# Queueing the first loads of the down projection in order of need, ahead of the last stores of the gate and up projections

## The chip, the cores and the metric

The kernel runs on one core of a Trainium2 chip. The metric is the device time of one execution in microseconds (us), the median of three runs. Besides it there is the profile of one execution; the times in its rows count from the start of its span.

## The reference, cut to what matters

One layer of a hybrid encoder: half a SwiGLU block, a mixing stage (attention beside a recurrent group), and half a SwiGLU block again. 1024 rows of a prompt and 64 rows of running streams go through together (1088 tokens, width 1024). What the change touches is the passage between the two halves of each SwiGLU block:

```python
def swiglu(x, w_gate, w_up, w_down):                 # 1024 -> 2816 -> 1024
    return (jax.nn.silu(x @ w_gate) * (x @ w_up)) @ w_down
x = x + 0.5 * swiglu(rms_norm(x, norm_ffn1), ffn1_gate, ffn1_up, ffn1_down)
...
x = x + 0.5 * swiglu(rms_norm(x, norm_ffn2), ffn2_gate, ffn2_up, ffn2_down)
```

## The kernel before, in words

Every product is made with operands split into a high and a low part (three passes of the matrix engine), and the two SwiGLU blocks use a seven-product scheme of the Winograd kind on 2x2 blocks, so each block of work has seven products where the plain one would have eight.

**Gate and up** (`gate_up`, lines 281 to 486). The seven combinations of the normalised input lie in SBUF as S0 to S6, each with a high and a low tile, in a pool on the right side of SBUF. 22 matrices are worked off, gate and up by turns; each takes its seven products in the order S0, S5, S4, S6, S1, S2, S3 (`UNIT`, line 225), 24 matmuls of 272 columns per product. `after` takes the results out of PSUM; after an up matrix the finished hidden pair is combined, split and stored to DRAM (`store`, to `hcd` and `hsd`). The last pair has no partner and is stored by `store_rows` (lines 436 to 450) to `hd`: for each of two halves one DMA of `hi` (line 448), one of `hs` (449) and one of `gt` (450).

**Down** (`Down`, lines 495 to 681). It runs over 5 groups of 7 blocks. A block needs one tile of hidden values `h` (1 MB, tags ha to he in rotation, `load_h`), one weight unit `wh`, made on chip by a cast (ScalarE) and a subtraction (VectorE) from a raw tile `dr` of 2 MB per group (two DMAs, `load_raw`) or from sums of its parts that GpSimd makes (lines 550 to 556), and, in blocks 0, 1, 3 and 4, the rows of the streams `hs` (0.25 MB per group, `load_hs`). A block is 24 matmuls of 512 columns, 28 with `hs`. Its results are added to the residual tiles x0 to x8 (`load_x`, 0.5 MB each, 0.25 MB for x8). The units lie in a ring of six: two in `whb` on the right, four in `whl` on the left. The weights of the last pair (`wr`, line 137) are loaded by the same `refill`.

**The turn.** In the last product of the last matrix (n = 6, S3) `run` of the matrix calls `last()`, which builds `Down`: it closes the pool of S and lays its own buffers where S was, so a load must wait for the last product that reads the S tiles beneath its buffer (a wait per tile, `reuse_waits="tile"`). Then come `after`, `store_rows`, the closing of gate_up's pools on the left, and `Down.run`, which lays further buffers where these were.

**What sets the order.** The program is written in one sequence, and a planner at build time simulates it and fixes the order on each engine: what it believes to be ready first is issued first. All loads and stores here are issued by SP, which takes them strictly in that order: an issue that waits for its data or its buffer holds back those behind it. Nothing in the kernel before ties the loads at the turn to each other or to the stores.

**Where the buffers lie.** The pools on the right grow from the high end downwards, and the first tile of a pool lies lowest. From the tile sizes (S: 8.5 KB per partition each, x: 4, dr: 16, h: 8, hs: 2):

| buffer | before: over | after: over |
|---|---|---|
| dr of group 0, dt | S5, S0 | S5, S0 |
| ha (h0) | S4, S5 | S4 |
| hb (h1) | S4 | S4, S2 |
| hc (h2) | S3, S4 | S2 |
| hs | gt and p1 (left side) | S4, S5 |
| x0, x1 | S0 | S0 |
| x8, x2 | S0 and S2, S2 | S1, S1 |
| x3 | S2 | S3, S1 |
| x4 to x7 | S2, S2 and S1, S1, S1 | S3 (x4 also S0) |
| hd, he (h3, h4) | gt, hi | hl, p1 (split weights) |
| dr of group 1 | hl, p1 | gt, p1 |
| whb | S6, S1 | S6, S1 |

The functions that the change touches, and those that call them:

Of the kernel before, what the change touches and what calls it, by code (L numbers as in the profile page):

```python
# [37 lines left out]
def rows(t):  # L38
    return 128 if t < 8 else NS


def build(tc, I, O):
# [15 lines left out]
    def left(name, bufs=1, **k):  # L58
        return Pool(name, bufs, side="left", reuse_waits="tile", **k)

    def right(name, bufs=1, **k):
        return Pool(name, bufs, side="right", reuse_waits="tile", **k)
# [30 lines left out]
    def bits(ap):  # L93
        return ap.bitcast(F32)
# [134 lines left out]

    def new_s(pool):  # L230
        made = {i: tuple(pool.tile([128, 4, 2, CW], F32R, tag=f"S{i}{b}") for b in "hl")
                for i in (3, 4, 5, 0, 2, 1, 6)}
        return [made[i] for i in range(7)]

    def build_s(p, a, b, S7, tmp, eng=None):
# [45 lines left out]
    def gate_up(tag, S7, turn, first=None, go=None):  # L281
# [62 lines left out]
        class Matrix:  # L344
# [51 lines left out]
            def run(self, ns, last=None):  # L396
                for n in ns:
                    product(*self.begin(n))
                    if n == 6 and last:
                        last()  # L400
                    self.after(n)
                if self.kind == "u":
                    (self.store if self.i < 2 * NG else self.store_rows)()

            def store(self):

# [88 lines left out]
    class Down:  # L495
        def __init__(self, tag, sP, keys, src):

            self.tag, self.src, self.w = tag, src, I["d" + tag]
            sP.close()
            open_ring(keys)  # L500
            self.xp = right("xd")
            self.right = [right(n) for n in ("dr", "dt", "dh")]
            rr, self.tp, hr = self.right
            self.raws, self.t, self.h, self.hs = {}, {}, {}, {}
            self.rawp, self.hp = {0: rr}, dict.fromkeys("abc", hr)
            ring["blocks"] = self.blocks
            order_x = (0, 1, 8, 2, 3, 4, 5, 6, 7)
            x = {t: self.xp.tile([128, D], tag=f"x{t}") for t in order_x}
            self.x = [x[t] for t in range(NT)]
            for i in (2, 1, 0):  # L510
                self.h_tile(i)
            self.load_raw(0)
            self.load_h(0)
            refill(1)
            self.load_h(1)
            refill(2)
            G.memset(self.x[8][NS:128], 0.0)
            for t in order_x[:5]:
                self.load_x(t)
            self.load_h(2)  # L520

        def load_x(self, t):
            SP.dma_start(self.x[t][:rows(t)], self.src[t * 128:t * 128 + rows(t), :])

        def load_raw(self, g):
            if g < NG:
                r = self.raws[g] = self.rawp[g % 2].tile([128, 2, 4, 512], tag="dr")
                for i in range(2):
                    SP.dma_start(r[:, i], self.w[2 * g + i])

        def h_tile(self, k):
            tag = "abcde"[k % 5]
# [2 lines left out]
        def load_h(self, k):  # L535
            if k < 7 * NG:
                if k not in self.h:
                    self.h_tile(k)
                SP.dma_start(bits(self.h[k]), hcd[k // 7, k % 7])

        def load_hs(self, g):
            if g < NG:
                h = self.hs[g] = self.hsp.tile([128, 4, 128], F32R, tag="hs", bufs=2)
                SP.dma_start(bits(h), hsd[g])

        def blocks(self, tag, g, i):
            r = self.raws[g]
# [13 lines left out]
        def run(self):  # L561
            x = self.x
            open_rest()
            self.left = [left(n) for n in ("dl", "ds", "de")]
            self.rawp[1], self.hsp, hl = self.left
            self.hp.update(dict.fromkeys("de", hl))
            vw = right("vw")
            acc = {n: [vw.tile([128, 512], tag=f"{n}{p}") for p in range(4)] for n in "vw"}
            ps = Pool("pw", 8, space=PSUM, reuse_waits="tile")
            self.load_hs(0)  # L570
            self.load_h(3)
            refill()
            self.load_h(4)
            for t in (4, 5, 6, 7):
                self.load_x(t)

            def bank():
                return ps.tile([128, 512], tag="pw")

            def add(out, p, scale, first=False):  # L580
                if first:
                    S.activation(out=out, in_=p, func=AF.Copy, scale=scale)
                else:
                    V.scalar_tensor_tensor(out=out, in0=p, scalar=scale, in1=out, op0=OP.mult, op1=OP.add)  # L584

            lo, hi = slice(0, 512), slice(512, 1024)

            def evac(g, i, p, q):
                v, w = acc["v"][p], acc["w"][p]
                if i == 0:  # L590
                    add(v, q, 0.5, g == 0)
                elif i == 1:
                    add(x[p][:, lo], q, 0.5)
                elif i == 2:
                    add(v, q, 0.5)
                elif i == 3:
                    add(w, q, 0.5, g == 0)
                elif i == 4:
                    add(x[p][:, hi], q, 0.5)
                elif i == 5:  # L600
                    add(w, q, -0.5)
                else:
                    add(x[p + 4][:, lo], q, 0.5)

            def sample(g, i, q):
                if i == 0:
                    add(x[8][:, hi], q, -0.5)
                elif i == 1:
                    add(x[8][:, lo], q, 0.5)
                elif i == 4:  # L610
                    add(x[8][:, hi], q, 0.5)

            for g in range(NG):
                self.load_hs(g + 1)
                for i in range(7):
                    h, u = self.h.pop(7 * g + i), units["s", self.tag, g, i]
                    begins = i in (0, 2, 3, 5)
                    if begins:
                        qs = {}
                    row = {0: 0, 1: 1, 3: 0, 4: 1}.get(i)  # L620
                    for p in [0, 1, 2, 3] + ([4] if row is not None else []):
                        if begins:
                            qs[p] = bank()
                        if p < 4:
                            seq = [(h[:, r, a, p * 128:p * 128 + 128], u[:, b, r * 512:r * 512 + 512])
                                   for r in range(2) for a, b in PASSES]
                        else:
                            seq = [(self.hs[g][:, 2 * r + row], u[:, b, r * 512:r * 512 + 512])
                                   for r in range(2) for b in range(2)]
                        for j, (l, m) in enumerate(seq):  # L630
                            PE.matmul(qs[p], l, m, start=begins and j == 0, stop=j == len(seq) - 1,  # L631
                                      skip_group_check=not begins)
                        if p < 4:
                            evac(g, i, p, qs[p])
                        else:
                            sample(g, i, qs[p])
                    del units["s", self.tag, g, i]
                    self.load_h(7 * g + i + 5)
                    refill()
                    if g == NG - 1 and i == 2:  # L640
                        for p in range(4):
                            G.tensor_tensor(out=x[p][:, hi], in0=x[p][:, hi], in1=acc["v"][p], op=OP.subtract)
                        for p in range(4):
                            G.tensor_tensor(out=x[p + 4][:, lo], in0=x[p + 4][:, lo], in1=acc["v"][p], op=OP.add)
                    if g == NG - 1 and i == 5:
                        for p in range(4):
                            G.tensor_tensor(out=acc["w"][p], in0=acc["w"][p], in1=acc["v"][p], op=OP.subtract)
                            G.tensor_tensor(out=x[p + 4][:, hi], in0=x[p + 4][:, hi], in1=acc["w"][p], op=OP.add)
                del self.hs[g]
            ps.close()  # L650
            for p in [vw] + self.right[::-1] + self.left[::-1]:
                p.close()
# [133 lines left out]
    def turn1():  # L786
        down[1] = Down("1", sP, down_keys("1") + [("r", j) for j in range(8)]
                       + [(p, j) for p in "kqv" for j in range(4)] + [("o", j) for j in (4, 5, 6, 7, 0, 1, 2, 3)],
                       I["x"])

    gate_up("1", S7, turn1, first1)
    d1 = down[1]
# [597 lines left out]

    def turn2():
        down[2] = Down("2", sP, down_keys("2"), xd)

    gate_up("2", S7, turn2, go=rest)
    d2 = down[2]
# [123 lines left out]
```

## Time and profile before

| | |
|---|---|
| time, median of 3 runs | 2104.07 us (2102.86 to 2110.48) |
| the profiled execution: its time | 2107.18 us |
| its span | 2105.3 us |
| TensorE busy | 1943.2 us (92%) |
| VectorE, ScalarE, GpSimd busy | 1416.7, 842.0, 756.0 us |
| mean granted TensorE clock | 0.968 of full |
| moved by DMA | 328.92 MB, mean 156 GB/s |
| the turns of the two SwiGLU blocks | about 518 us and 1823 us |

How to read the rows: PE is the matrix engine, PEld its weight loads, DVE is VectorE, ACT ScalarE, POOL GpSimd, SPq the queue of SP. A timeline row gives start, duration, engine, line, operation, output<-input and how many were merged; in square brackets the idle time of the engine before it and what ended that. [...]

### The profile page before, as it was taken

Reading aid. Unit: us, or ns where it says so; the run is one execution under the profiler, and the core shown is the slowest. Engines: PE = TensorE matmul, PEld = TensorE weight load, DVE = VectorE, ACT = ScalarE, POOL = GpSimd, SP = SyncE. Lnnn points to the kernel's source line nnn. Section 1 sums busy time; section 2 is a strip of 40 time slices with the busy share of each in tenths; the row PEclk is TensorE's granted clock in tenths of the full one; section 3 lists DMA queues with packets and bytes.
Section 4 is the critical chain, followed back from the end, with each engine's and each line's share of the span. In section 5 each row is a group of like instructions: output and inputs, shape, how many; then the busy total and the mean of one; then the engine's idle time right before and its main releaser. Section 6 shows DMA issues by size and latency. Waiting matters only on the chain.

```text
span 2105.3 us, 32015 instructions
## 1 busy us (share of the span) xinstructions
PE 1943.2 (92%) x12260; PEld 1764.9 (84%) x12260; DVE 1416.7 (67%) x2420; ACT 842.0 (40%) x1604; POOL 756.0 (36%) x561
## 2 busy tenths in 40 slices
PE   4999999998499999998998988799999999749999
PEld 3999999998388879986876866699999999738887
DVE  7777677665367767168944877866677767437774
ACT  7534344443121124356762766544344434221110
POOL 5654444442312151013121422454444444322213
PEclk9999999999699999998999999899999999979999
DMA  3243344333965552214369953333344333485652
GB/s 127 82 158 139 114 162 150 139 113 128 362 227 217 180 178 101 83 57 129 104 191 249 179 125 100 125 125 142 113 162 150 139 113 145 166 332 220 226 211 85
DMA packets 130812, 328.92 MB, mean 156 GB/s; under 512 B 19074, under 2 KB 73762, under 8 KB 112995
## 3 DMA queue, kind: packets, MB, share of 16 engines
q1 hardware_dynamic: 109922, 312.45, 42.0%
q0 software_dynamic: 20736, 14.42, 4.2%
q8 instruction: 97, 1.59, 0.3%
q14 instruction: 57, 0.46, 0.1%
HBM read 208.85 MB, written 117.98 MB: 155 GB/s over the span
## 4 chain that ended last, share of the span: by engine, by line
PE 49%; DMA 5%; DVE 5%; ACT 3%; issue 1%; SPq 0%; ACTq 0%; DVEq 0%
PE pq L331 22%; PE pw L631 10%; PE pg L219 5%; PE pg L1046 4%; PE pd L675 2%; PE T L1234 2%; PE T L1223 2%; PE S L1175 1%; DMA x<-xd 1%; DMA hs<-hsd 1%; DMA ot<-od 1%; DMA hb<-hcd 1%; PE T L1208 1%; DVE xs L197 1%; DMA hd<-gt 1%
## 5 line engine op out<-in xcount | busy, mean ns | idle before, releaser
L420 DVE TENSOR_TENSOR hi<-gt,hi 128x512 fp32r<-128x512 f32 x140 | 165.1, 1179 | 40.4 <-ACT hi L419 38.7
L98 DVE TENSOR_TENSOR hl<-t,hl 128x512 fp32r<-128x512 f32 x132 | 106.9, 810 | 125.7 <-ACT hl L97 124.6
L98 DVE TENSOR_TENSOR hl<-raw,hl 128x512 fp32r<-128x512 f32 x176 | 170.3, 969 | 9.6 <-ACT hl L97 9.5
L584 DVE SCALAR_TENSOR_TENSOR x<-pw,x 128x512 f32<-128x512 f32 x150 | 101.7, 688 | 111.2 <-PE pw L631 110.7
L97 ACT CAST hl<-raw 128x512 fp32r<-128x512 f32 x176 | 108.9, 621 | 117.9 <-PE pq L331 76.9
L419 ACT CAST hi<-gt 128x512 fp32r<-128x512 f32 x140 | 85.4, 621 | 167.5 <-DMA hcd<-hi 90.5
L331 PE MATMUL pq<-S0h,hl 128*128 128x272 f32 x704 | 143.3, 292 | 5.2 <-ACT hl L97 4.2
L331 PE MATMUL pq<-S1h,hl 128*128 128x272 f32 x704 | 140.4, 288 | 3.2 <-ACT p L463 3.2
L1046 PE MATMUL pg<-wh,xh 128*128 128x512 f32 (+1 forms) x432 | 140.3, 404 | 0.0
L331 PE MATMUL pq<-S5h,hl 128*128 128x272 f32 x704 | 139.9, 288 | 0.0
L331 PE MATMUL pq<-S4h,hl 128*128 128x272 f32 x704 | 139.5, 287 | 0.0
L331 PE MATMUL pq<-S6h,hl 128*128 128x272 f32 x704 | 139.4, 287 | 0.0
L331 PE MATMUL pq<-S2h,hl 128*128 128x272 f32 x704 | 139.4, 287 | 0.0
L331 PE MATMUL pq<-S3h,hl 128*128 128x272 f32 x704 | 139.4, 287 | 0.0
L331 PEld LDWEIGHTS pq<-S0h,hl 128*128 128x128 f32 x704 | 115.7, 192 | 5.9 <-ACT hl L97 4.6
L331 PEld LDWEIGHTS pq<-S1h,hl 128*128 128x128 f32 x704 | 113.6, 188 | 3.8 <-ACT p L463 3.8
L331 PEld LDWEIGHTS pq<-S5h,hl 128*128 128x128 f32 x704 | 113.5, 188 | 0.0
L331 PEld LDWEIGHTS pq<-S6h,hl 128*128 128x128 f32 x704 | 113.3, 188 | 0.0
L331 PEld LDWEIGHTS pq<-S4h,hl 128*128 128x128 f32 x704 | 113.3, 188 | 0.0
L331 PEld LDWEIGHTS pq<-S3h,hl 128*128 128x128 f32 x704 | 113.3, 188 | 0.0
L331 PEld LDWEIGHTS pq<-S2h,hl 128*128 128x128 f32 x704 | 113.3, 188 | 0.0
L304 POOL TENSOR_TENSOR t<-t,raw 128x512 f32<-128x512 f32 x44 | 58.8, 1336 | 133.3 <-DVE hl L98 133.3
(285 smaller groups left out, 5531.7 us busy)
## 6 DMA issues: line engine op xcount, KB each, us to landing
hcd<-hi SPq DMA_DIRECT2D x140, 512.0 KB, 2.7
raw<-in_g SPq DMA_DIRECT2D x22, 1024.0 KB, 6.1
raw<-in_u SPq DMA_DIRECT2D x22, 1024.0 KB, 5.0
dr<-in_d SPq DMA_DIRECT2D x20, 1024.0 KB, 8.3
ha<-hcd SPq DMA_DIRECT2D x14, 1024.0 KB, 4.8
hb<-hcd SPq DMA_DIRECT2D x14, 1024.0 KB, 4.8
hc<-hcd SPq DMA_DIRECT2D x14, 1024.0 KB, 4.9
hd<-hcd SPq DMA_DIRECT2D x14, 1024.0 KB, 4.8
```

Source lines behind the costliest of these rows:

```text
L97: S.copy(out=hi, in_=raw)
L98: (eng or V).tensor_tensor(out=lo, in0=raw, in1=bits(hi), op=OP.subtract)
L219: PE.matmul(p[:, :n], w[:, a, k, :], x2[b][:, k, o:o + n], start=i == 0, stop=i == 23)
L304: G.tensor_tensor(out=t2, in0=t2, in1=r[:, 2], op=OP.add)
L331: PE.matmul(q[:, c, :CW], h[:, a, k * 128:k * 128 + 128], S7[i][b][:, k, c, :], start=start and j == 0, stop=j == 11, skip_group_check=not ...
L419: S.copy(out=hi, in_=v)
L420: V.tensor_tensor(out=lo, in0=v, in1=bits(hi), op=OP.subtract)
L584: V.scalar_tensor_tensor(out=out, in0=p, scalar=scale, in1=out, op0=OP.mult, op1=OP.add)
L631: PE.matmul(qs[p], l, m, start=begins and j == 0, stop=j == len(seq) - 1, skip_group_check=not begins)
L675: PE.matmul(p, l, r, start=i == 0, stop=i == len(seq) - 1)
L1046: PE.matmul(ps[:n], x2[b][:, 2 * j + kk, ts], w[:, a, kk, :], start=half == 0 and i == 0, stop=half == 1 and i == 11)
L1223: PE.matmul(po[:n, :128], aT[:kw, i, :n], v[:kw, vi[i], :], start=i == 0, stop=i == nk - 1)
```

## The change

The loads of `Down.__init__` and the first of `Down.run` go through a new method `queue`, which ties each to the one before by `tc.issue_after`: it sets the order of issue on SP and adds no wait for the earlier transfer. The order is dr (two), h0, hs, x0, x1, h1, x8, x2, x3 in `__init__`, then h2, h3, h4, x4 to x7 in `run`. The last load of `__init__` is handed back as `gate`, and `store_rows` is traced under `issue_after(gate)`, so its six DMAs are issued behind x3's load. From then on (`ordered = False`) loads are as free as before; the first full `refill`, with the load of dr of group 1, is moved behind x4 to x7. `hs` goes to the right side, `dl` and `de` on the left change places, the order of the S tiles and of the x tiles in memory changes (table above). No instruction of arithmetic is added or taken away.

```diff
     def new_s(pool):
...
-                for i in (3, 4, 5, 0, 2, 1, 6)}
+                for i in (2, 4, 5, 0, 3, 1, 6)}
...
                     if n == 6 and last:
-                        last()
+                        gate = last()
                     self.after(n)
-                if self.kind == "u":
-                    (self.store if self.i < 2 * NG else self.store_rows)()
+                if last:
+                    with tc.issue_after(gate):
+                        self.store_rows()
+                elif self.kind == "u":
+                    self.store()
...
-            self.right = [right(n) for n in ("dr", "dt", "dh")]
-            rr, self.tp, hr = self.right
+            self.right = [right(n) for n in ("dr", "dt", "ds", "dh")]
+            rr, self.tp, self.hsp, hr = self.right
...
-            order_x = (0, 1, 8, 2, 3, 4, 5, 6, 7)
-            x = {t: self.xp.tile([128, D], tag=f"x{t}") for t in order_x}
+            x = {t: self.xp.tile([128, D], tag=f"x{t}") for t in (0, 1, 4, 5, 6, 7, 3, 8, 2)}
...
+            self.gate = None
             self.load_raw(0)
             self.load_h(0)
             refill(1)
+            G.memset(self.x[8][NS:128], 0.0)
+            self.load_hs(0)
+            for t in (0, 1):
+                self.load_x(t)
             self.load_h(1)
             refill(2)
-            G.memset(self.x[8][NS:128], 0.0)
-            for t in order_x[:5]:
+            for t in (8, 2, 3):
                 self.load_x(t)
-            self.load_h(2)
+
+        def queue(self, out, src):
+
+            if not self.ordered:
+                return SP.dma_start(out, src)
+            if self.gate is None:
+                self.gate = SP.dma_start(out, src).ins
+                return
+            with tc.issue_after(self.gate):
+                i = SP.dma_start(out, src)
+            self.gate = i.ins
...
-            self.left = [left(n) for n in ("dl", "ds", "de")]
-            self.rawp[1], self.hsp, hl = self.left
+            self.left = [left(n) for n in ("de", "dl")]
+            hl, self.rawp[1] = self.left
...
-            self.load_hs(0)
+            self.load_h(2)
             self.load_h(3)
-            refill()
             self.load_h(4)
             for t in (4, 5, 6, 7):
                 self.load_x(t)
+            self.ordered = False
+            refill()
```

In `load_x`, `load_raw`, `load_h` and `load_hs` the call `SP.dma_start` becomes `self.queue`. `turn1` and `turn2` return `down[1].gate` and `down[2].gate`.

## Rows read from the trace of the kernel before

**Rows 1.** The page, busy time of TensorE over the span, and its granted clock in 40 slices of the span, in tenths.
```profile
PE 1943.2 (92%) x12260; PEld 1764.9 (84%) x12260; DVE 1416.7 (67%) x2420; ACT 842.0 (40%) x1604; POOL 756.0 (36%) x561
...
PEclk9999999999699999998999999899999999979999
```

**Rows 2.** Busy time by windows around the first turn: from:to, length, then PE, PEld, DVE, ACT, POOL busy us with the count of instructions, granted clock, DMA share, GB/s.
```profile
500.00:550.00 50.00, 32.02 (x193) 28.20 (x191) 23.93 (x23) 12.08 (x17) 14.43 (x6) 0.85 0.64 244
550.00:600.00 50.00, 30.63 (x122) 25.07 (x123) 16.85 (x21) 8.61 (x10) 9.45 (x4) 0.74 0.68 266
```

**Rows 3.** Windows again, of the matmuls of down (line 631) alone: first turn, steady running, second turn. Columns: length, PE and PEld busy with counts, granted clock, DMA share, GB/s.
```profile
518.09:605.23 87.14, 49.79 (x193) 39.74 (x194) 0.76 0.82 317
...
650.00:700.00 50.00, 50.00 (x222) 41.44 (x221) 1.00 0.52 185
...
1823.43:1904.65 81.22, 42.79 (x169) 34.13 (x170) 0.79 0.82 314
```

**Rows 4.** Windows of all engines over the parts of each turn, columns as in rows 2.
```profile
518.09:529.52 11.43, 0.00 (x0) 0.03 (x1) 5.11 (x7) 3.18 (x4) 2.38 (x2) 0.63 0.97 371
529.52:544.88 15.36, 13.93 (x48) 10.31 (x48) 12.00 (x8) 5.95 (x8) 9.73 (x3) 0.83 1.04 378
544.88:569.37 24.49, 0.00 (x1) 0.00 (x1) 1.48 (x3) 0.00 (x0) 4.68 (x2) 0.57 1.02 418
...
1823.43:1835.07 11.64, 0.00 (x0) 0.03 (x1) 5.11 (x7) 3.18 (x4) 2.38 (x2) 0.71 0.95 372
...
1850.47:1875.01 24.54, 0.00 (x0) 0.00 (x1) 1.45 (x3) 0.00 (x0) 4.68 (x2) 0.60 1.02 418
```

**Rows 5.** Timeline of PE at the first turn, the rows with waits.
```profile
529.52 0.77 PE L631 MATMUL pw<-wh,ha 128*128 128x512 f32 x1 [11.44 <-DMA ha<-hcd]
...
540.50 4.38 PE L631 MATMUL pw<-wh,hb 128*128 128x512 f32 x18 [1.17 <-ACT v L582]
569.37 2.08 PE L631 MATMUL pw<-wh,hs 128*128 128x512 f32 x4 [24.49 <-DMA hs<-hsd]
```

**Rows 6.** Timeline of SP's queue at the first turn: when each DMA was issued (the durations are those of the issues).
```profile
517.76 0.32 SPq L448 DMA_DIRECT2D hd<-hi  x1
518.17 1.21 SPq L529 DMA_DIRECT2D dr<-in_d  x2
...
520.47 4.30 SPq L523 DMA_DIRECT2D x<-in_x  x5
...
536.78 0.37 SPq L450 DMA_DIRECT2D hd<-gt  x1
537.85 1.76 SPq L529 DMA_DIRECT2D dr<-in_d  x2
...
551.08 1.55 SPq L529 DMA_DIRECT2D dr<-in_d  x2
...
554.87 0.33 SPq L544 DMA_DIRECT2D hs<-hsd  x1
```

**Rows 7.** Waits of SP's queue from 440 to 520 us: who was waited for, total us, times, longest.
```profile
SPq L448 <- ACT hs L444: 25.2, 1, 25.2
```

**Rows 8.** The matmuls from 496 to 519 us that read S5, S4, S1 and S2 (high tiles): least, mean and greatest ns of one, and the time from the first start to the last.
```profile
L331 PE MATMUL pq<-S5h,hl x16: 283/288/290, 499.9 to 502.8; 128*128 128x272 f32 x16
...
L331 PE MATMUL pq<-S4h,hl x16: 283/287/290, 502.9 to 505.8; 128*128 128x272 f32 x16
...
L331 PE MATMUL pq<-S1h,hl x16: 283/287/290, 508.9 to 511.8; 128*128 128x272 f32 x16
...
L331 PE MATMUL pq<-S2h,hl x16: 283/287/290, 511.9 to 514.8; 128*128 128x272 f32 x16
```

**Rows 9.** Timeline of the first turn: the clearing of half of x8, and the making of weight units on ScalarE, VectorE and GpSimd.
```profile
515.21 0.95 POOL L517 MEMSET x<- 64x1024 f32 x1 [3.83 <-PE pq L331]
...
527.00 1.99 ACT L97 CAST wh<-dr 128x1024 fp32r<-128x1024 f32 x2 [5.34 <-DMA dr<-in_d]
...
528.08 5.71 DVE L98 TENSOR_TENSOR wh<-dr,wh 128x1024 fp32r<-128x1024 f32 x2 [5.17 <-ACT wh L97]
...
537.15 1.23 DVE L98 TENSOR_TENSOR wh<-t,wh 128x1024 fp32r<-128x1024 f32 x1 [3.36 <-ACT wh L97]
...
551.13 2.34 POOL L550 TENSOR_TENSOR t<-dr 128x1024 f32<-128x1024 f32 x1 [9.38 <-DMA dr<-in_d]
```

**Rows 10.** DMA issues from 515 to 600 us by kind: count, KB each, median us from issue to landing.
```profile
dr<-in_d SPq DMA_DIRECT2D x6, 1024.0 KB, 11.3
x<-in_x SPq DMA_DIRECT2D x8, 512.0 KB, 12.7
...
hb<-hcd SPq DMA_DIRECT2D x2, 1024.0 KB, 11.9
...
hd<-hi SPq DMA_DIRECT2D x2, 512.0 KB, 7.2
hd<-gt SPq DMA_DIRECT2D x2, 512.0 KB, 10.1
wr<-in_d SPq DMA_DIRECT2D x2, 512.0 KB, 12.6
hs<-hsd SPq DMA_DIRECT2D x3, 256.0 KB, 15.4
```

**Rows 11.** The page, the same for the loads of raw gate and up weights over the whole run.
```profile
raw<-in_u SPq DMA_DIRECT2D x22, 1024.0 KB, 5.0
```

More of the change, by code (lines that the diff above doesn't have):

```diff
@@ L498, in __init__ @@
             self.tag, self.src, self.w = tag, src, I["d" + tag]
+            self.ordered = True
             sP.close()
@@ L514, in __init__ @@
             refill(1)
+            G.memset(self.x[8][NS:128], 0.0)
+            self.load_hs(0)
+            for t in (0, 1):
+                self.load_x(t)
             self.load_h(1)
             refill(2)
-            G.memset(self.x[8][NS:128], 0.0)
-            for t in order_x[:5]:
+            for t in (8, 2, 3):
                 self.load_x(t)
-            self.load_h(2)
+        def queue(self, out, src):
[7 more added lines that the diff above has]
+            self.gate = i.ins
         def load_x(self, t):
-            SP.dma_start(self.x[t][:rows(t)], self.src[t * 128:t * 128 + rows(t), :])
+            self.queue(self.x[t][:rows(t)], self.src[t * 128:t * 128 + rows(t), :])
         def load_raw(self, g):
@@ L528, in load_raw @@
                 for i in range(2):
-                    SP.dma_start(r[:, i], self.w[2 * g + i])
+                    self.queue(r[:, i], self.w[2 * g + i])
         def h_tile(self, k):
@@ L538, in load_h @@
                     self.h_tile(k)
-                SP.dma_start(bits(self.h[k]), hcd[k // 7, k % 7])
+                self.queue(bits(self.h[k]), hcd[k // 7, k % 7])
         def load_hs(self, g):
@@ L543, in load_hs @@
                 h = self.hs[g] = self.hsp.tile([128, 4, 128], F32R, tag="hs", bufs=2)
-                SP.dma_start(bits(h), hsd[g])
+                self.queue(bits(h), hsd[g])
         def blocks(self, tag, g, i):
@@ L789, in turn1 @@
                        I["x"])
+        return down[1].gate
     gate_up("1", S7, turn1, first1)
@@ L1392, in turn2 @@
         down[2] = Down("2", sP, down_keys("2"), xd)
+        return down[2].gate
     gate_up("2", S7, turn2, go=rest)
```

## The prediction, made before the result was known

> **What bounds the kernel now.** I read the page first: TensorE is busy 92% of the span, and its granted clock is at full speed except in a few slices, two of them near 0.25 and 0.88 of the span [rows 1]. The windows show what happens there: in the 100 us around the first turn TensorE is busy only 62.65 us, at a granted clock of 0.85 and 0.74 [rows 2]. How much each turn loses comes from the windows of line 631 [rows 3]. In steady running 222 matmuls take 50.00 us, 0.225 us each. From the end of the last gate/up product to 605.23 there are 193 in 87.14 us: 43.5 us of work, 43.7 us lost. The second turn has 169 in 81.22 us: 38.1 of work, 43.2 lost. Together 86.9 us, the most this change can give back.
>
> The loss has three parts [rows 4]. TensorE stands still for 11.43 us before the first block, and for 24.49 us after the second; the second turn has 11.64 and 24.54. [...] The PE timeline says who ended each wait: the load of ha the first, the load of hs the second, and ScalarE's copy of v a third of 1.17 us [rows 5].
>
> SP's queue explains both loads. dr of group 0 was issued at 518.17, right behind the store of hi, and hs only at 554.87, behind five tiles of x, the last stores, dr of group 1 and even dr of a later group [rows 6]. SP had waited 25.2 us for the store of hi, whose data ScalarE made [rows 7]; nothing was in transfer meanwhile that the turn needs. During the long wait DMA moves 418 GB/s with a share of 1.02 [rows 4]: the transfers themselves are then the bound, and the order decides what comes first.
>
> **The change, part by part.** I work on the first turn, from the end of gate/up at 518.09; the second has the same rows within 0.3 us.
>
> *First loads earlier.* dr of group 0 lies over S5 and S0. The last reads of S5 start near 503, of S4 at 506, of S1 at 512, of S2 at 515 [rows 8]. That a buffer really comes free tile by tile is shown by the clearing of x8, which in the kernel before lies over S2: it began at 515.21, released by PE, three us before PE ended [rows 9]. So dr can be issued at 503 instead of 518.17, h0 and hs at 506, x0 and x1 with them. These are 2.10 + 1.05 + 0.26 + 1.05 = 4.5 MB [rows 10], 10.7 us at 418 GB/s; a load of 1 MB that meets little else lands 5.0 us after its issue [rows 11]. dr is in by about 511 and all of these by 515, beside products that need no DMA.
>
> *First weight units earlier.* The unit needs its buffer in whb, free with S1 at 512, a cast of 1.0 us and a subtraction of 1.23 us, or half of 5.71 us while GpSimd works [rows 9]: ready at 514 to 516, before 518.1. The next three units wait for GpSimd's three sums, 2.34 us each, and are wanted at the third block, 12.6 us after the turn. So the 11.4 us go. What is late next is the hand-over of PSUM and of v from gate_up's last evacuations; I put 0.5 us, between 0 and the 2.8 us that lay between dr's landing and the steady stream before (527.0 to 529.5, rows 5 and 9).
>
> *hs and the stores.* hs leaves the left side, so it no longer waits for gt's store (issued 536.78 [rows 6]), and stands fourth in order. The 24.5 us go, and with both stalls the time at the lower clock. The six stores lose their place ahead of dr: the hi of the first half goes from 517.76 to behind x3, which waits for S3's end at 518.1. Nobody in down reads hd until its very end. But dr of group 1 now lies over gt and waits for the stores: wanted only for the eighth block at 559, less 9.3 us for its three sums, cast and subtraction [rows 9], so by 550.
>
> *The queue behind.* From 515 SP issues h1, x8, x2 and x3, 2.35 MB; then, as ready, h2, h3, h4, x4 to x7 and the stores, 7.4 MB. At 418 GB/s the 9.8 MB are in by 538.5. Blocks take 28 x 0.225 = 6.3 us with hs and 5.4 without: they begin at 518.1, 524.4, 530.7, 536.1, 542.4, 548.7, 554. h1 (518), h2 (525), h3 (530) and h4 (534) are in time. The planner orders the rest freely: h5, dr of group 1 and wr, 4.2 MB, bring it to 548.5. h5 is wanted at 548.7: no slack if it comes last of these, 7.5 us of slack if first, and if dr of a later group (issued at 551.08 before [rows 6], 2.1 MB) is ahead too, 5 us late. I take 2 us, between 0 and 5, nearer the early side because h5's buffer is free as soon as block 0 ends, at 524.4.
>
> [...]
>
> *ScalarE.* Block 1 adds onto block 0's banks, so it waits for the copies of v, which stood behind casts that waited for GpSimd: 1.17 us before [rows 5]. GpSimd now starts earlier, but so does the block. I take 1.5 us, between 0 and 2.4 us, twice the row.
>
> *Sum.* Left per turn: 0.5 + 2 + 1.5 = 4 us, bounds 0 and 10.2. Gain: 86.9 - 8 = 79 us, bounds 66 and 87. From the profiled execution's 2107.2 us (its span of 2105.3 and 1.9 around it) that gives 2028; the median of the runs is 3.1 us lower, which gives 2025. I predict 2027; bounds by the same sum 2017 to 2041.
>
> **The rivals.**
>
> *A new queue at the turn.* What stood first in line was hs; now dr of group 1, held by gt's stores, may hold SP while h5 and h6 stand behind it. For it: the free order before put a later group's dr and wr ahead of hs [rows 6], and a landing took 10 to 15 us under load [rows 10]. Against: there are about 30 us between x3's issue and the first need. A stall of 8 to 15 us per turn, with the clock after it, leaves 2045 to 2062.
>
> *The early loads don't come early.* If dr still goes out at about 518, by a wait that the planner puts ahead of it or a buffer that comes free later than I read, the 11.4 us stay with their share of the lower clock, about 15 us per turn, and the gain is some 27 us per turn: 2052, or up to 2085 if hs is also late by half. Against it stands the clearing of x8 at 515.21 [rows 9].
>
> *Slower.* The place is TensorE's own order, also fixed by the planner. If it puts a block at PE's head whose load ends up last in SP's line, all of the 20.5 MB that moved from 518 to 569 must pass first (49 us at 418 GB/s). It decides from the point at which this load lands later than 518.1 + 43.5 = 561.6 with one block done at most: 49 us against the 43.5 lost now is 5.5 us per turn, 2115 us. Against it: the loads up to x7 are now chained, so the only candidates are the unchained ones.
>
> **How the numbers follow.** The forecast (2017 to 2041) 70%; the new queue 16%; loads not early 8%; the chain without effect on what bounds, within 10 us of before, 3%; slower 3%. The range 2016 to 2060 leaves out about 15% at the top and little below, since 2017 is the gain without any rest. A measurement of this kernel tells about 0.5%, 10.5 us, from no change: faster 0.94, same 0.03, slower 0.03.
>
> **What would show it.** SP: dr issued near 503, hs near 506, stores behind x3 at 518 or later. PE: no wait over 2 us from 518 to 560, the granted clock 1.00 in all windows of both turns, 193 matmuls of line 631 in about 47 us. ScalarE's first cast of a unit before 515. Wrong would be: a wait of line 631 for a DMA of more than 5 us, dr issued after 515, or a saving at the turns that comes back later as waits in the first group. Whether the planner's order follows the listing is the step that I know least about.

## The result, and the profile after

The changed kernel takes 2044.26 us, median of four runs (2042.0 to 2046.68), beside 2104.24 us for the kernel before on the same chip: a ratio of 0.971 with a 95% interval of 0.9685 to 0.9734. A second measurement, run r1 below, gave 0.9704 [0.9689, 0.9718]. The profiled span went from 2105.3 to 2044.7 us, 60.6 us less. The forecast was 2027 us, so 17 us of the gain that I counted on did not come.

The page of after, the lines that answer to [rows 1]:
```profile
PE 1938.2 (95%) x12260; PEld 1762.8 (86%) x12260; DVE 1416.5 (69%) x2420; ACT 840.8 (41%) x1604; POOL 752.9 (37%) x561
...
PEclk9999999999899999998998999899999999999999
```
TensorE's work is the same 12260 matmuls. The two low slices of the clock (6 and 7) have become 8 and 9. The windows of down's matmuls (now line 649) over the first turn, in steady running and over the second turn answer to [rows 3], with the same columns:
```profile
518.09:609.66 91.57, 81.72 (x345) 66.68 (x345) 0.94 0.84 327
650.00:700.00 50.00, 50.00 (x222) 41.42 (x221) 1.00 0.48 172
1794.07:1884.83 90.76, 81.45 (x349) 66.63 (x350) 0.96 0.85 330
```
The steady rate is still 50.00 / 222 = 0.2252 us per matmul. The first turn does 345 in 91.57 us, 77.7 us of work and 13.9 lost; the second 349 in 90.76, 78.6 of work and 12.2 lost. Before, 43.7 and 43.2 us were lost. The difference is 86.9 - 26.1 = 60.8 us, all of the gain. So the loss at the turns was the right place to look. Of the 26 us still left there the forecast had 8; the other 18 are what it missed.

SP's queue of after at the first turn, answering to [rows 6]:
```profile
502.93 0.33 SPq L533 DMA_DIRECT2D dr<-in_d  x1
503.32 0.42 SPq L536 DMA_DIRECT2D dr<-in_d  x1
506.06 0.33 SPq L536 DMA_DIRECT2D ha<-hcd  x1
506.44 0.43 SPq L536 DMA_DIRECT2D hs<-hsd  x1
...
515.33 2.96 SPq L536 DMA_DIRECT2D x<-in_x  x3
519.80 0.33 SPq L451 DMA_DIRECT2D hd<-hi  x1
...
527.08 0.56 SPq L536 DMA_DIRECT2D hc<-hcd  x1
...
539.79 1.55 SPq L531 DMA_DIRECT2D dr<-in_d  x2
...
544.38 1.00 SPq L531 DMA_DIRECT2D dr<-in_d  x2
```
dr of group 0 goes out at 503 instead of 518.17, hs at 506.44 instead of 554.87, and the first store of hi stands behind x3. The reader should also note the two last rows: the dr at 539.79 is that of group 2, and dr of group 1, which is needed first, goes out behind it; ScalarE's first cast of group 1 waits for this later one until 562.64 (row below, in the part on the prediction).

SP's waits show one thing more about the order. In the trace of before, 20 of the 23 issues from 524.44 to 558.68 began within 0.25 us of the landing of the DMA issued eight places before them (for the other three the trace has no such landing). That of hs, at 554.87, is one of them (SP's waits of before, 552 to 556 us):
```profile
SPq L544 <- DMA x<-in_x: 0.9, 1, 0.9
```
The load of x issued at 543.14 had landed at 554.85, while the last store of gt, which hs's buffer waited for, had landed at 545.80. So in that stretch SP had at most eight transfers under way, and a load started when its place in the order came up, even where its buffer had long been free. That sharpens the reading of [rows 6]: hs was late by its place, 9 us more than by gt's store.

The loads are early, and still TensorE waits. Its timeline, the first rows of down and every row with a wait until 600 us, answering to [rows 5]:
```profile
525.60 0.80 PE L649 MATMUL pw<-wh,ha 128*128 128x512 f32 x1 [7.55 <-ACT wh L97]
527.04 8.22 PE L649 MATMUL pw<-wh,ha 128*128 128x512 f32 x23 [0.64 <-DVE wh L98]
...
573.45 5.55 PE L649 MATMUL pw<-wh,hc 128*128 128x512 f32 x23 [1.69 <-DVE wh L98]
```
No wait of TensorE for a DMA is left. The first block waits 7.55 us for ScalarE's cast of the first weight unit (line 97), and then for VectorE's subtraction. The timeline of ScalarE shows why:
```profile
506.07 0.61 ACT L374 COPY u<-pq 128x544 f32<-128x544 f32 x1 [4.88 <-PE pq L331]
518.73 1.04 ACT L446 CAST hi<-gt 128x1024 fp32r<-128x1024 f32 x1 [12.05 <-DVE gt L359]
...
523.41 1.04 ACT L446 CAST hi<-gt 128x1024 fp32r<-128x1024 f32 x1 [3.50 <-issue]
...
524.51 1.99 ACT L97 CAST wh<-dr 128x1024 fp32r<-128x1024 f32 x2
```
ScalarE stands idle for 12.05 us in front of the cast of the last stores (line 446), which waits on VectorE for the evacuation of gate_up's last product but one (`after(5)`); the second cast of the stores then waits for the one of the last product (`after(6)`). The casts of the weight units stand behind both of these casts in its queue. Their data was there: GpSimd began to add parts of the same dr at 513.20 (rows below).

Windows of all engines over the parts of the first turn, answering to [rows 4]:
```profile
518.09:525.60 7.51, 0.00 (x0) 0.00 (x0) 5.20 (x6) 3.38 (x6) 2.71 (x1) 0.80 1.00 354
525.60:545.00 19.40, 18.75 (x68) 14.92 (x69) 14.88 (x16) 7.91 (x10) 3.33 (x1) 0.81 1.01 389
545.00:571.37 26.37, 26.37 (x119) 21.81 (x117) 10.38 (x15) 4.40 (x6) 4.81 (x2) 1.00 1.01 418
571.37:577.00 5.63, 3.94 (x17) 2.92 (x16) 5.38 (x6) 1.04 (x1) 1.26 (x1) 1.00 0.55 199
```
Of the 13.9 us lost, 7.51 are the wait, 19.40 - 68 x 0.2252 = 4.1 are what follows it, 0.64 of them the wait for the subtraction and the rest mostly the lower clock (0.81), and 5.63 - 17 x 0.2252 = 1.8 the wait at block 7. From 545 on TensorE runs at its steady rate beside 418 GB/s of DMA.

### The profile page after: what moved, and what is told of

Its sections match the earlier page's. It is cut to its first block, busy times and chain, and to the rows that moved or that the text cites. A ratio compares the mean times of both kernels' runs of the same rounds, so it can differ in the third digit from the quotient of the medians.

```text
span 2044.7 us, 32014 instructions
## 1 busy us (share of the span) xinstructions
PE 1938.2 (95%) x12260; PEld 1762.8 (86%) x12260; DVE 1416.5 (69%) x2420; ACT 840.8 (41%) x1604; POOL 752.9 (37%) x561
## 4 chain that ended last, share of the span: by engine, by line
PE 81%; DVE 9%; DMA 4%; ACT 3%; issue 1%; SPq 0%; DVEq 0%; ACTq 0%
PE pq L331 45%; PE pw L649 21%; PE pg L219 5%; PE pg L1065 2%; PE pd L693 2%; PE T L1253 2%; PE T L1242 2%; PE S L1194 2%; DMA x<-xd 1%; DVE xs L197 1%; PE pg L1253 1%; DVE wh L98 1%; DMA ot<-od 1%; PE T L1227 1%; DVE xc L980 0%
```

## The experiments

Every run was timed against the kernel before on the same chip (medians of 2106 to 2108 us). The "idle" column is the time TensorE stood waiting ahead of down's matmuls, over both turns, added up over each profile (before: 75.8; after: 19.2).

| run | edit to | us | ratio, 95% interval | idle |
|---|---|---|---|---|
| r1 | after itself | 2045.05 | 0.9704 [0.9689, 0.9718] | 19.6 |
| r4 places alone | after | 2063.08 | 0.9792 [0.9776, 0.9808] | 33.1 |
| r11 chain, stores free | after | 2064.62 | 0.98 [0.9785, 0.9814] | 31.3 |
| r5 hs alone | before | 2099.05 | 0.9967 [0.9955, 0.9979] | 66.5 |
| r10 S and x in old places | after | 2048.16 | 0.972 [0.9704, 0.9737] | 20.7 |
| r2 units ahead of the stores' casts | after | 2052.94 | 0.974 [0.9726, 0.9755] | 21.3 |
| r3 and ahead of the last evacuation | r2 | 2055.05 | 0.975 [0.9736, 0.9765] | 21.7 |
| r6 dr of group 1 before group 2 | after | 2058.24 | 0.9776 [0.9761, 0.979] | 25.8 |
| r7 both | r3, r6 | 2048.3 | 0.9728 [0.9713, 0.9742] | 17.5 |
| r8 and ahead of the last two evacuations | r7 | 2045.94 | 0.972 [0.9704, 0.9736] | 17.4 |
| r9 v before later units | r8 | 2047.76 | 0.9721 [0.9706, 0.9735] | 20.8 |
| r12 h2 before the stores | r9 | 2039.43 | 0.9688 [0.9675, 0.9701] | 12.8 |

For r1: 

> The changed kernel once more, beside the three below on the same chip. 2042 to 2047 us, a ratio of 0.969 to 0.973 to the kernel before. First block of down 7.5 us after the end of gate/up at both turns.

It came out so; the first block starts after 7.55 us of waiting at both turns.

**Which part of the change made the gain.** r4 takes out the chain and the gate. It keeps the places, and with them what the listing moved (the load of hs behind that of h0, the first full `refill` behind x4 to x7):
```diff
-                with tc.issue_after(gate):
-                    self.store_rows()
+                self.store_rows()
...
-            self.ordered = True
+            self.ordered = False
```


> The buffers as in the changed kernel, but no load is tied to another and the stores are free. The planner's order on SP then differs in one place only: the first store of hi stands ahead of dr. Theory (with the casts behind store_rows, the early dr is worth little: what counted was hs's place): dr is issued near 518 to 520 and lands 524 to 526, PE starts 9 to 11 us after gate/up, hs causes no wait; total 2047 to 2056 us. Rival (my prediction's sum: the early loads are worth 11 us and some clock per turn by themselves): 2066 to 2076 us.

The time came out between the two. r11 keeps the chain and frees the stores only (the first half of that diff):

> after, with the chain of loads kept but the last stores free (no gate on them). Theory: the chain alone puts nothing where it was not; the first store of hi goes ahead of dr again and holds SP until ScalarE and VectorE have made it, so the first block waits 11 us for ha and the time is that of r4 (places alone), 2060 to 2066. Rival: the chain of loads is what brought the 18 us between r4 and after, and the gate nothing: 2044 to 2052.

The rows of r11 from SP's queue and from TensorE's timeline:
```profile
518.08 0.32 SPq L450 DMA_DIRECT2D hd<-hi  x1
518.49 0.38 SPq L532 DMA_DIRECT2D dr<-in_d  x1
```
```profile
530.56 0.77 PE L648 MATMUL pw<-wh,ha 128*128 128x512 f32 x1 [12.15 <-DMA ha<-hcd]
```
The store of hi is ahead of dr again, and block 0 waits 12.15 us for ha, as before the change and as expected. r4 and r11 have the same time within their intervals. So the chain of loads alone gives nothing; the gate, which holds the stores back, is worth the 18 us between r4 and r1 (9 per turn), in the presence of the chain. Whether the gate would do it without the chain was not run.

r5 gives the kernel before one thing, hs on the right and its load behind that of h0:
```diff
-            self.right = [right(n) for n in ("dr", "dt", "dh")]
+            self.right = [right(n) for n in ("dr", "dt", "ds", "dh")]
...
             self.load_h(0)
             refill(1)
+            self.load_hs(0)
```


> The kernel before with one thing changed: hs lies on the right and is loaded after h0; no chain, the other places as before. Theory (the place of hs is the larger part of the gain): no wait for hs, the start 11 us late as before, hd and he perhaps late since they still lie over gt; total 2052 to 2070 us. Rival (another load takes the place of hs, as its buffer or its turn comes too late): a wait of 10 us or more for hd or he at each turn, total 2080 to 2100 us.

The theory fell and the rival came. The wait for hs is gone, and its successor is nearly as long, in TensorE's timeline of r5:
```profile
571.88 7.56 PE L631 MATMUL pw<-wh,hd 128*128 128x512 f32 x24 [21.64 <-DMA hd<-hcd]
```
hd (h3) lies over gt here, as hs did, and is issued only at 556.09, behind the stores and the loads of dr of groups 1 and 2. As with hs before, it was its place in the order that held it: the last store of gt went out at 536.95 and so had landed at about 546 (an estimate, with the 9.02 us that the same store took in before), and eight places ahead of hd's issue stands a load of x, as ahead of that of hs. In after hd lies over the split weights, since `dl` and `de` have changed places, and the `refill` with dr of group 1 stands behind its load. hs gives 7 us alone, everything that r4 keeps 44 (2107.22 - 2063.08). r10 puts the S and x tiles back into their old order:
```diff
-                for i in (2, 4, 5, 0, 3, 1, 6)}
+                for i in (3, 4, 5, 0, 2, 1, 6)}
...
-            x = {t: self.xp.tile([128, D], tag=f"x{t}") for t in (0, 1, 4, 5, 6, 7, 3, 8, 2)}
+            x = {t: self.xp.tile([128, D], tag=f"x{t}") for t in (0, 1, 8, 2, 3, 4, 5, 6, 7)}
```


> after, with the S tiles and the x tiles laid in the order of before (hs on the right, dl and de exchanged, chain and gate stay). Theory: what the layout is worth comes from hs and from the exchange of dl and de; S and x in their old order only move which of S1, S2, S3 a load of x or h1 waits for, a few us in a queue that has them. The time is 2042 to 2050, the start wait of 7.55 us for ScalarE's cast stays, and no wait for a DMA over 1.5 us appears before block 4. Rival: the order of S and x was needed for h2 (here over S3, free at 518 instead of S2 at 515), and block 2 waits for it by 3 us or more at the lower clock: 2052 to 2065.

As expected: 0.972 against 0.9704, intervals that overlap. So, with chain and gate present, the order of S and x is worth at most a few us, and the 44 us are left to hs, the exchange and the moved `refill` together. Which of the last two brought hd forward was not run.

**What the left 26 us are.** The theory: the wait of 7.55 us is an order on ScalarE, not a lack of data. r2 puts the last stores' casts and subtractions behind those of the second unit (`split` hands back its two instructions, `refill` keeps the last pair in `ring["made"]`):
```diff
-                with tc.issue_after(gate):
+                act, dve = ring["made"]
+                with tc.issue_after(gate), tc.issue_after(act), tc.issue_after(dve):
                     self.store_rows()
```


> store_rows is also tied behind the first two weight units on ScalarE and VectorE, no more. Theory (the first unit is late because ScalarE takes its cast only after the casts of store_rows, which wait for the last product's results; dr itself landed by 513): the casts start at 512 to 513 instead of 524.5; the first subtraction stays behind the last product's two evacuations on VectorE, so PE starts 2.5 to 3.5 us after the end of gate/up instead of 7.5. Here dr of group 1 is issued later than in the changed kernel, behind he, which can cost 3 to 6 us per turn at block 7. Total 2036 to 2044 us. Rival (the start is held by the hand-over of PSUM and v from gate_up, or by dr): the wait stays at 7 us or more, total 2044 or more.

The two places are seen side by side in TensorE's timeline of r2:
```profile
517.92 0.40 PE L650 MATMUL pw<-wh,ha 128*128 128x512 f32 x1
522.67 1.65 PE L650 MATMUL pw<-wh,ha 128*128 128x512 f32 x3 [4.35 <-DVE wh L98]
...
571.16 1.51 PE L650 MATMUL pw<-wh,hc 128*128 128x512 f32 x4 [4.47 <-ACT wh L97]
```
The wait for the cast is gone, down begins at 517.92, so the order on ScalarE was the cause of that wait; the 4.35 us behind it are VectorE's subtraction, as expected. But the time is 8 us longer than that of after. The windows of down's matmuls from 518 to 560 and from 560 to 620, first of after, then of r2, show where it went:
```profile
518.00:560.00 42.00, 33.75 (x134) 27.34 (x135) 0.88 1.01 395
560.00:620.00 60.00, 58.31 (x257) 47.92 (x256) 1.00 0.72 283
```
```profile
518.00:560.00 42.00, 37.65 (x156) 30.68 (x156) 0.92 1.02 403
560.00:620.00 60.00, 54.33 (x225) 43.50 (x224) 0.94 0.65 258
```
r2 is 22 matmuls (5.0 us) ahead at 560 and 10 behind at 620. In its queue dr of group 1 went out only at 556.21, behind dr of group 2 and other loads:
```profile
556.21 0.90 SPq L532 DMA_DIRECT2D dr<-in_d  x2
```
So block 7 waits 4.47 us, as the expectation had named it, and the clock drops again (0.94). r3 also moves gate_up's last evacuation, `after(6)`, behind the units:

> As the run before, and the evacuation of the last product is tied behind the two units too. Theory: unit 0 is ready at 516 to 518, PE starts within 1 us of the end of gate/up, with the granted clock at 1.00; the late dr of group 1 still costs 3 to 6 us per turn at block 7. Total 2024 to 2036 us. Rival (hand-over of PSUM): with the evacuation later, the start is as late as before or later, total 2044 or more.

Neither came: the start wait fell only to 3.70 us (now VectorE's subtraction alone), and block 7 waited 5.28, the same exchange as in r2. The time lies where the rival had it, but the start is not as late as the rival says.

r6 leaves the units and orders the queue: the stores chained behind x3, the later loads behind them, dr of group 1 chained, dr of group 2 held behind it.
```diff
-                    self.queue(r[:, i], self.w[2 * g + i])
+                    if g != 2:
+                        self.queue(r[:, i], self.w[2 * g + i])
+                        continue
+                    with tc.issue_after(self.gate):
+                        SP.dma_start(r[:, i], self.w[2 * g + i])
```


> The changed kernel, and besides: the six stores and dr of group 1 stand in the chain (x3, stores, h2 to h4, x4 to x7, dr of group 1), and dr of group 2 behind it. Theory (block 7 waits because dr of group 2 goes ahead of group 1): the waits of 1.7 and 1.1 us for a unit at block 7 go, the start stays 7.5 us late; total 2039 to 2044 us. Rival (the unit is late by the order on VectorE whatever dr does): 2044 to 2047 us.

Both were off, by 11 us and more. The wait at block 7 is gone, but block 8 has one of 4.7 us in both turns. Rows of VectorE and of TensorE in r6:
```profile
574.71 6.70 DVE L98 TENSOR_TENSOR wh<-dr,wh 128x1024 fp32r<-128x1024 f32 x2
581.33 2.47 DVE L606 SCALAR_TENSOR_TENSOR v<-pw,v 128x512 f32<-128x512 f32 x4
```
```profile
582.11 4.57 PE L653 MATMUL pw<-wh,hd 128*128 128x512 f32 x12 [4.71 <-issue]
```
The two subtractions of later units took 6.70 us beside GpSimd's sums (2.35 alone), and the additions to v stood behind them. Block 8 adds onto the banks that these read, and TensorE goes on at 582.11, 0.8 us after the first began. The profile names no releaser ("issue"), so this last link is read from the times, not shown. The waits of r6 are 6.6 us longer than those of after, and its time 13 us; the clock is down again behind block 8 (0.91 from 580 to 600), and the rest of the difference was not traced.

r7 and r8 join r3 and r6; r8 also moves `after(5)` behind the units:

> Run r3 with the chain of run r6. Theory: the 5.3 us for the unit at block 7 and the slower clock after them were what ate r3's gain; PE starts with a wait of 3.7 us for the first subtraction, which VectorE takes up only at 518.6; total 2029 to 2036 us. Rival (the earlier start is given back later by VectorE or ScalarE): 2042 or more.

> As r7, and the evacuations of the last two products stand behind the two subtractions on VectorE. Theory: subtractions from 513 to 519, PE goes from gate/up into down with a wait under 1 us and the clock granted at 1.00, no wait over 2 us up to block 7; total 2016 to 2026 us, near the 2020 that the stalls at the turns were worth in all. Rival (hand-over of PSUM): the start is held by the late evacuations for 3 us or more, total 2030 or more.

r7 still waits 3.71 us for the subtraction at both turns and 5.72 for a unit at block 8 of the second, so its rival was right. In r8 TensorE goes from gate/up into down without any wait, and the time is nevertheless where the rival had it, by another mechanism: not the start is held but block 1. Its rows from TensorE and ScalarE:
```profile
529.14 7.35 PE L661 MATMUL pw<-wh,hb 128*128 128x512 f32 x24 [4.46 <-ACT v L612]
```
```profile
524.71 1.04 ACT L97 CAST wh<-t 128x1024 fp32r<-128x1024 f32 x1
525.66 1.99 ACT L97 CAST wh<-dr 128x1024 fp32r<-128x1024 f32 x2
527.55 1.04 ACT L97 CAST wh<-t 128x1024 fp32r<-128x1024 f32 x1
528.50 2.04 ACT L612 ACTIVATE v<-pw 128x512 f32<-128x512 f32 x4
```
Block 1 adds onto the banks that ScalarE must first copy to v, and four casts for blocks 2 to 5 stand ahead of that copy. At block 8 of the second turn, 5.58 us are lost for a unit, as in r7. r9 puts the four casts behind the copies of v (`self.v` is the last copy; the `refill` at the head of `run` goes):
```diff
+                    if (g, i) == (0, 0):
+                        self.ordered = True
+                        with tc.issue_after(self.v):
+                            refill()
+                        self.ordered = False
                     refill()
```


> r8 with ScalarE's copies of v of block 0 put ahead of the casts of units 2 to 5 (the refill at the head of run comes behind block 0, and its instructions are issued behind the last copy of v). Theory: at each turn 4.5 us were given back in r8 by these casts alone, which stood ahead of the copies that block 1 waits for. Then the wait of block 1 (4.46 us in r8, both turns) falls to under 0.8 us, the last-pair stage after the first turn begins 3 to 4 us earlier than in r8 (736.60), near 733, and the time is 2034 to 2041. Rival: the units of group 1 (GpSimd's three sums, casts, subtractions) set the pace from block 7 on, because the landing of dr of group 1 does not move; then the wait at block 7 or 8 grows by as much as block 1's shrinks, and the time stays at 2043 to 2048.

Block 1's wait fell to 0.68 us as expected, but the time stayed where the rival had it, and again by another mechanism: not blocks 7 and 8 took over the wait but block 2, by TensorE's timeline and SP's queue of r9:
```profile
537.93 8.01 PE L660 MATMUL pw<-wh,hc 128*128 128x512 f32 x24 [6.51 <-DMA hc<-hcd]
```
```profile
527.63 0.75 SPq L544 DMA_DIRECT2D hc<-hcd  x1
```
h2 is issued behind the six stores, at 527.63, where after has it too (527.08): there it was hidden by the late start. r12 moves its load into the first chain:
```diff
             for t in (8, 2, 3):
                 self.load_x(t)
+            self.load_h(2)
...
-            self.load_h(2)
             self.load_h(3)
```


> r9 with the load of h2 (hc) moved into the chain of Down's first loads, right behind x3, so that it is issued ahead of the six last stores (in r9 it was issued behind them at 527.63 and block 2 waited 6.51 and 5.36 us for it). Theory: each order of the planner that is put right shows the next wait, and h2 behind the stores was the next; h2's buffer is free at 515, so it lands before 530, no wait at block 2 is left, block 2's matmuls run at 1.00, and the last-pair stage after the first turn begins at 732 to 736 (739.60 in r9, 740.22 in after). The time is 2032 to 2042, the first one clearly below after's 2045. Rival: the pace from block 7 on is set by the landing of dr of group 1 (558.0 in r9) with GpSimd's sums and VectorE's subtractions behind it, so that the 6 us come back as waits at blocks 7 and 8; then 2043 to 2049.

The time came out as expected, and block 2 waits no more: 0.9688 [0.9675, 0.9701] over five runs. Its slowest run (2041.48) is below every run of after (2042.0 to 2046.85), but they were not run side by side and the intervals overlap a little, so a gain of 3 to 5 us over after is likely and not proved. Windows of line 660 in r12 at the two turns:
```profile
518.09:609.66 91.57, 85.19 (x365) 69.17 (x364) 0.98 0.87 340
1788.00:1878.00 90.00, 83.60 (x359) 68.13 (x358) 0.98 0.87 340
```
Lost are 91.57 - 365 x 0.2252 = 9.4 us and 90.00 - 359 x 0.2252 = 9.2, instead of 13.9 and 12.2: 7.5 us of the 9.5 by which the profiled spans differ (2035.2 and 2044.7). What waits now are h3, issued behind the stores (2.59 and 1.63 us), and VectorE at blocks 7 and 8 (up to 4.09 us).

## Why the prediction was right in sign and short in size

*What bounds.* Right: the 86.9 us lost at the turns were the whole field, and 60.8 of them came back. The three waits that I named make 11.43 + 24.49 + 1.17 = 37.1 of the first turn's 43.7; the other 6.6 lie in work at a lower clock, granted at 0.83 between the two long waits [rows 4] and at 0.91 from 569.37 to 605.23, with small waits in it.

*First loads earlier.* Right to the microsecond: dr at 502.93 (503 predicted), h0 and hs at 506. GpSimd used dr at 513.20, right behind the clearing of x8; I had it landed by 511.

*First weight units earlier: the step that failed.* I had the unit "ready at 514 to 516" and concluded "So the 11.4 us go". The cast began at 524.51, the subtraction at 525.77. I had counted when the buffer is free and the data there, and left out the third condition, the instruction's turn on its engine. The planner had put the cast of the last stores first on ScalarE, and ScalarE stood idle for 12.05 us in front of it and took the unit's cast, which stood behind, only afterwards. In r8, where the unit's cast stands first, it starts at 512.20. The signs named beforehand said so too: TensorE has a wait of more than 2 us before 560, and ScalarE's first cast of a unit, due before 515, came 9.5 us late. Of the wait of 11.43 us [rows 4] only 3.9 went, and with the 7.51 that stayed the lower clock behind it stayed too: 7.51 + 4.1 = 11.6 us in the first turn, where my sum had 0.5 for the start. r2, r3 and r8 show the cause by taking the wait away. That the forecast would have come true without this wait is not shown, and the runs speak against it: r8 has no wait at the start and takes 2045.94 us, as after does, because block 1 and then block 8 wait instead. The late unit hid terms of the sum that were too small as well (next paragraphs).

*hs and the stores.* Right: no wait for hs in either turn. That hd must come earlier as well, which r5 shows, I had not seen; the diff did it. I gave gt's store as what held hs; its place among eight transfers under way held it 9 us longer.

*The queue behind.* The size fits, 2 us taken and 1.8 measured in the first turn (a wait of 1.69, and 1.12 in the second), but by luck. h5 came in time, and block 7 waited. I had named dr of a later group as the one that might go ahead, and dr of group 2 did; dr of group 1 was there only at 562.64, where I had it by 548.5, or 5 us later behind dr of group 2. Rows of ScalarE and of VectorE in after:
```profile
562.64 2.01 ACT L97 CAST wh<-dr 128x1024 fp32r<-128x1024 f32 x2 [8.62 <-DMA dr<-in_d]
```
```profile
572.17 2.35 DVE L98 TENSOR_TENSOR wh<-dr,wh 128x1024 fp32r<-128x1024 f32 x2
```
At the forecast's pace block 7 begins at 559 and would have waited 3.6 us for this data alone (an estimate from the two times, with the landing left where it is); the late start covered that. What it did wait for in after was VectorE's subtraction, which came at 572.17, behind additions to x. So this too is a place in an engine's queue; r6, with dr of group 1 earlier, has the subtraction at 568.98 and no such wait. 418 GB/s held for 26.37 us, as assumed.

*ScalarE's copies of v.* 1.5 us taken, no wait measured in after. They matter once the start is early: 4.46 us in r8, more than the 2.4 that was my bound. (The second turn of before already had 1.99 us here, not 1.17; the "same rows within 0.3 us" do not hold for this one.)

*The rivals.* 2044 lies just under the window of "a new queue at the turn", 2045 to 2062, but that mechanism did not occur: no wait of TensorE for a DMA is in the trace at either turn. The forecast's own range, 2017 to 2041, missed; the whole range held the time. No step of the slower case occurred (its 20.5 MB come to 20.3 by [rows 4], on which nothing rests).

## What to carry to other kernels

The first unit's cast had its data and its buffer by 511.97, where r3 starts it, and its turn on ScalarE at 524.51 in after. So there are three times to write down for each engine in the chain: when the data is there, when the buffer is free, and when the instruction's turn comes. Where orders are fixed at build time, undoing the first bad order shows the next (cast, subtraction, copy of v, h2, h3 here), and one alone may cost time, as in r2, r3 and r6: count the matmuls done by several fixed moments, not only the wait that went. A gate that holds a blocking store back can be worth more than the order of the loads behind it: 18 us against nothing here (r1, r4 and r11).

## What the runs showed of the hardware

Operations of VectorE with both inputs in SBUF took up to 3.9 times as long here while GpSimd added tensors (2.80 us against 0.72). Rows of VectorE and of GpSimd in after:
```profile
511.38 0.72 DVE L359 TENSOR_TENSOR gt<-u,gt 128x544 f32<-128x544 f32 x1 [1.48 <-POOL u L379]
...
515.09 0.72 DVE L386 TENSOR_TENSOR u<-pq,u 128x544 f32<-128x544 f32 x1 [2.28 <-PE pq L331]
515.85 2.80 DVE L359 TENSOR_TENSOR gt<-u,gt 128x544 f32<-128x544 f32 x1
...
525.77 2.35 DVE L98 TENSOR_TENSOR wh<-dr,wh 128x1024 fp32r<-128x1024 f32 x2
```
```profile
513.20 2.40 POOL L567 TENSOR_TENSOR t<-dr 128x1024 f32<-128x1024 f32 x1
515.68 2.39 POOL L568 TENSOR_TENSOR dr<-dr 128x1024 f32<-128x1024 f32 x1
```
An operation of line 359 takes 0.72 us at 511.38, with GpSimd at rest; the same form took 2.80 at 515.85 and ended 0.58 us after GpSimd's sum of 515.68. Its neighbour at 515.09, which reads one input from PSUM, kept 0.72 beside a running sum. Two subtractions of units take 2.35 us alone, 4.50 in r3 and 6.70 in r6 beside sums. The early loads made GpSimd's sums early too (513.20, against 527.06 in before), and beside them that step of the evacuation of gate_up's last product but one took the 2.80 us; in before it took 0.72, at 515.88, with no sum running. The stores' cast and behind it the unit's cast waited for it; that loss I had not priced.

The other thing is what a stop costs behind itself. In after the first block's 24 matmuls took 0.80 + 8.22 us after 7.51 us at rest, the clock granted at 0.50 from 525.60 to 532.00; in r8, without the rest, they took 5.63, near the 5.60 of its blocks from 540 to 560 at a clock of 1.00. Block 1 of r8, after 4.46 us at rest, took 7.35, the clock at 0.91 from 520 to 540.
